# Six buffers for the evictions of one projection unit, and one array for the parked operands of the last units

## The chip, the cores and the metric

The kernel runs on one core of a Trainium2 chip. The metric is the device time of one execution in microseconds; where there are several runs, their median counts. A profile is one execution recorded by the hardware. Its span goes from the first to the last instruction, and the time of the same execution is a little longer.

## What is computed

One inference layer of a streaming encoder, for a prompt of 2048 frames and for 64 frames of a running stream with 4096 past frames. Cut to what matters here:

```python
def layer_inputs(x, norm_g, w_in, b_gate, qn_g, kn_g):
    h = rmsnorm(x, norm_g) @ w_in
    qa, ka, va, za, qb, kb, vb, zb, ga, gb = jnp.split(h, _split_points(), axis=-1)
...
    oa = diff_attn_prompt(qa, ka, va, lam, slopes)
    ob, r_p = retention_prompt(qb, kb, vb, log_g)
    hp = layer_output(hp, oa, ob, za, zb, ga, gb, subln_g[l], lam_init, w_o_diff[l], w_o_ret[l], w_out[l])
```

`h` has 6144 columns. `layer_output` gates the two branches, projects each to 1024 columns, merges them, projects once more and adds `x`.

## The kernel before, in words

**Tiling.** Every matmul operand is split into a high part in the fast format and a low part with the remainder, and each product is made of three matmuls: high by high, high by low, low by high. The prompt is projected in two halves of about 1024 frames. The first half, to about 585 us, uses a Strassen scheme over pairs of blocks. The second half uses, in this order, plain units of 256 columns (`transposed`: weights stationary, frames moving, result with columns on partitions; the first such unit has groups of 256 and 288 frames, the others of 512 and 288), units for k, q and v, and for the last five column groups seven products per group, again after Strassen (`quad`, about 1410 to 1544 us). Attention (`attn_head`: products `s<-K,q`, softmax, `pv<-ath,V`) and the retention steps (`ret_block`: loads `row<-qbT`, `row<-kbT` and `row<-vbN`, then `s<-row`) are interleaved with the second half. After that come the output projections, to the end.

**What sets the order.** The program is written by a planner. Each piece of work is a Python generator that issues instructions and yields the planned time at which it can go on; `loop` takes the ready task with the lowest priority number, and if none is ready it lets the planned TensorE time run forward. The planner adds estimated costs (`P`, `A`, `V`, `G`, `ld`, `st`). TensorE, ACT (ScalarE) and DVE (VectorE) execute in the order in which the planner writes; SP (SyncE, which issues almost all DMAs) and POOL (GpSimd) in the order that the framework makes of it, each a strict queue. Buffers have tags with a fixed number each: `take` waits for the earliest free one, `give` returns it with the time at which it is free. "ev" has three buffers, "tlo" two and "thi" one, all of 128x512.

**What the change touches.** `fin_t` (L1451) evicts a group of a `transposed` unit: it takes a buffer from `q_ev` (L1601), copies the group from its PSUM bank on ACT (`q_copy`, recorded at L1596), returns the bank, stores the buffer to DRAM on SP and returns the buffer when the store should have landed. `mm` has two PSUM banks, so TensorE cannot begin a group before the group two earlier has been copied. The first unit of the second half has eight groups, four of 256 and four of 288 frames; its stores go to `qbT`.

`x_again` (L1480) prepares the operands of the last units while the plain units run. In 20 chunks it forms on POOL the blocks of x (A21, A22, A11, A12 in a "tlo" buffer, called `xa`) and their Strassen sums (S1, S3, S4, S2 in a "thi" buffer, called `xs`), and parks what the seven products need in DRAM: three blocks, three sums, and S2 already split into high and low part. The split goes to a third buffer, an "ev": cast on ACT (L1498), subtraction on DVE (L1503). `x_pass` (L1515) later loads the parked arrays, S2's two parts first, and splits the others itself. `self.parked` becomes 1 when all chunks are parked; from then on `q_ev` may also take "thi" and "tlo".

Of the kernel before, what the change touches and what calls it, by code (L numbers as in the profile page):

```python
# [8 lines left out]
F32 = mybir.dt.float32  # L9
F32R = mybir.dt.float32r  # L10
# [30 lines left out]
SLACK = 400.0  # L41
PACE = 700.0
LATE = 1000.0
# [26 lines left out]


PLAIN = 11
SPREAD = 4000.0
PHASES = [("t2", "S2", "q_p6"), ("b11", "A11", "q_p1"), ("b21", "A12", "q_p2"), ("t1", "S1", "q_p5"),
          ("t3", "S3", "q_p7"), ("t4", "A22", "q_p4"), ("b22", "S4", "q_p3")]
NAMES = ("S1", "S3", "S4", "A22", "A11", "A12")
WIDTH = (256, 288)


# [93 lines left out]
class Hybrid:  # L173
# [123 lines left out]
    def scratch(self):  # L297
        tc = self.tc
        self.qT = [tc.dram_tile([4, 128, TT], F32, name=f"qT{i}") for i in range(2)]
        self.kT = [tc.dram_tile([4, 128, TT], F32, name=f"kT{i}") for i in range(2)]  # L300
        self.vN = [tc.dram_tile([TT, 512], F32, name=f"vN{i}") for i in range(2)]
        self.vsN = tc.dram_tile([NS, 512], F32, name="vsN")
        self.vbN = tc.dram_tile([TT, 512], F32, name="vbN")
        self.qbT = tc.dram_tile([4, 128, TT], F32, name="qbT")
        self.kbT = tc.dram_tile([4, 128, TT], F32, name="kbT")
        self.zaT = tc.dram_tile([4, 128, 8 * GW], F32, name="zaT")
        self.zbT = tc.dram_tile([4, 128, 8 * GW], F32, name="zbT")
        self.gaT = tc.dram_tile([8, 128, 8 * GW], F32, name="gaT")
        self.gbT = tc.dram_tile([8, 128, 8 * GW], F32, name="gbT")
        self.oaT = tc.dram_tile([4, 128, 8 * GW], F32, name="oaT")  # L310
        self.obT = tc.dram_tile([4, 128, 8 * GW], F32, name="obT")
        self.swap = tc.dram_tile([2, 4, 64, 1024], F32, name="swap")
        self.xkeep = tc.dram_tile([128, KC, 128], F32, name="xkeep")
        self.wsum = tc.dram_tile([16, 2, 128, 4, 256], F32, name="wsum")
        self.xd = tc.dram_tile([128, 6, 4, 544], F32, name="xd")
        self.xd2 = tc.dram_tile([128, 2, 4, 544], F32, name="xd2")
        self.mT = tc.dram_tile([8, 2, 128, 8, 128], F32, name="mT")

    def consts(self):
# [1160 lines left out]
    def x_again(self):  # L1480

        nc = self.nc
        yield lambda: "nat1" in self.done
        for g, w in enumerate(WIDTH):
            n = (128, 96)[g]
            for c, a in [(c, a) for c in range(4) for a in range(0, w, n)]:
                yield from self.take("tlo")
                yield from self.take("thi")
                raw, sums = (self.sb(self.ep, [128, 512], tag, name)[:, 0:4 * n].rearrange("p (k t) -> p k t", k=4)
                             for tag, name in (("tlo", "xa"), ("thi", "xs")))  # L1490
                t, t2 = self.x_chunk(g, c, raw, sums, a, n)
                usl = slice(256 * g + a, 256 * g + a + n)
                yield t
                t = self.st(self.xd[:, 3:6, c, usl], raw[:, 1:4], n << 11)
                yield t2
                ev, tag = yield from self.q_ev(2 * n)
                e = ev.bitcast(F32R).rearrange("p (k t) -> p k t", k=2)
                nc.scalar.copy(e[:, 0], sums[:, 3])  # L1498
                t3 = self.A(n, self.pe)
                self.give("tlo", max(t, t2))  # L1500
                t4 = self.st(self.xd[:, 0:3, c, usl], sums[:, 0:3], n << 11)
                yield t3
                nc.vector.tensor_sub(e[:, 1], sums[:, 3], e[:, 0].bitcast(F32))  # L1503
                t = self.V(n + 100, t3)
                self.give("thi", max(t, t4))
                yield t
                self.kept = self.st(self.xd2[:, :, c, usl], e.bitcast(F32), n << 10)
                self.give(tag, self.kept)
                yield self.pe + SPREAD
        self.parked = 1  # L1510

# [3 lines left out]
    def x_pass(self):  # L1515
        self.xslots, self.xfree, self.parked, self.xraw = [], [(1, 0.0)], -1, None
        yield lambda: self.parked == 1 and self.seg1_done is not None
        yield max(self.seg1_done, self.kept)
        for k, (_, name, _) in enumerate(PHASES):
            if k == 0:  # L1520
                for j, x in enumerate(self.x_slot(0)):
                    t = self.ld(x.bitcast(F32), self.xd2[:, j].rearrange("p c t -> p (c t)"), 1114112)
                self.xslots.append((0, t))
                yield lambda: self.xraw is not None
                continue
            t = self.ld(self.xraw, self.xd[:, NAMES.index(name)].rearrange("p c t -> p (c t)"), 1114112)
            s = yield from self.ring(self.xfree)
            yield t
            h, l = self.x_slot(s)
            for c in range(0, 2176, 544):  # L1530
                self.nc.scalar.copy(h[:, c:c + 544], self.xraw[:, c:c + 544])
                t = self.A(544, self.pe)
                yield t
                self.nc.vector.tensor_sub(l[:, c:c + 544], self.xraw[:, c:c + 544], h[:, c:c + 544].bitcast(F32))
                t = self.V(644, t)
            self.xslots.append((s, t))
            yield t
# [61 lines left out]
        return self.A(n, t)  # L1599

    def q_ev(self, n):  # L1601
        tag = yield from self.either(1, "ev", *(("thi", "tlo") if self.parked == 1 else ()))
        return self.sb(self.ep, [128, 512], tag, "ev")[:, :n], tag

    def q_p6(self, q, ps, bank, t, dst, d0, scale, grouped):
# [1601 lines left out]
```

## Time and profile before

| what | value |
|---|---|
| median of 3 runs | 1906.45 us (1902.84 to 1911.58) |
| the profiled execution's own time | 1899.9 us |
| its span | 1897.5 us |
| mean granted TensorE clock | 0.997 |
| busy: TensorE, DVE, ACT, POOL | 1871.9, 1336.5, 973.7, 670.7 us |
| DMA over the span | 340.09 MB, mean 179 GB/s |

Of the profiled execution, 2.4 us lie outside its span. Matmuls overlap: one of 128x288 lasts 0.29 us, but the next starts 0.13 us later. So idle time counts only where TensorE's last matmul has ended. "wh" and "wl" are the high and low part of a weight, "xh" and "xl" of the frames. A number in square brackets in a timeline is the engine's idle time just before the instruction, with what ended it. SPq is SP's queue, and its times are those of issuing a DMA, not of the transfer.

### The profile page before, as it was taken

What the parts mean: (1) busy time and instruction counts of PE and PEld (TensorE: products, weight loads), DVE (VectorE), ACT (ScalarE), POOL (GpSimd) and SP (SyncE); (2) the same over time, 40 slices, a digit from 0 to 9 for tenths busy, and PEclk for the clock granted to TensorE, in tenths of its full rate; (3) what the DMA queues carried; (4) which work ended last, traced back from release to release, by engine and by line L of the source; (5) the groups of instructions that cost most, each with busy time, mean ns of one, the idle gap of its engine ahead of it and who ended that gap; (6) DMA issues with size and microseconds to landing.
All of it is one profiled execution on the core that took longest, in us unless ns stands there. A gap on an engine that the chain in (4) does not pass through costs nothing.

```text
span 1897.5 us, 33103 instructions
## 1 busy us (share of the span) xinstructions
PE 1871.9 (99%) x11090; PEld 1649.4 (87%) x11090; DVE 1336.5 (70%) x3112; ACT 973.7 (51%) x2266; POOL 670.7 (35%) x728
## 2 busy tenths in 40 slices
PE   9999999999998999999999999999999999999999
PEld 7788888888877889888888889899999999999887
DVE  6765757657584777885467677578887969877664
ACT  6434544545434665655455555466666536654221
POOL 2420355554552122121311444431113635522442
PEclk9999999999999999999999999999999999999999
DMA  7664555666757857554622856753534998976542
GB/s 260 209 177 126 162 153 187 179 198 197 249 180 191 233 180 197 158 172 126 189 81 76 224 138 166 177 161 95 136 123 148 279 250 273 274 235 202 177 156 78
DMA packets 402876, 340.09 MB, mean 179 GB/s; under 512 B 85649, under 2 KB 348945, under 8 KB 401682
## 3 DMA queue, kind: packets, MB, share of 16 engines
q1 hardware_dynamic: 402706, 337.98, 60.9%
q8 instruction: 88, 1.44, 0.3%
q14 instruction: 82, 0.67, 0.1%
HBM read 218.27 MB, written 118.75 MB: 178 GB/s over the span
## 4 chain that ended last, share of the span: by engine, by line
PE 88%; DVE 5%; DMA 4%; issue 1%; ACT 1%; SPq 1%; POOL 1%; DVEq 0%; ACTq 0%
PE mm L1138 29%; PE mm L990 8%; PE tp L990 4%; PE at L1996 3%; PE s L1884 2%; PE s L1885 2%; PE s L990 2%; PE mm L1569 2%; PE pv L1976 2%; PE pv L1975 2%; PE pv L1974 2%; PE s L2800 1%; PE s L2799 1%; PE s L2798 1%; SPq L280 1%
## 5 line engine op out<-in xcount | busy, mean ns | idle before, releaser
L749 POOL TENSOR_TENSOR wl<-ws,wh 128x512 fp32r<-128x512 f32 x107 | 149.6, 1409 | 251.8 <-ACT wh L728 243.9
L1138 PE MATMUL mm<-wh,xh 128*128 128x512 f32 x504 | 203.7, 404 | 0.0
L1138 PE MATMUL mm<-wl,xh 128*128 128x512 f32 x504 | 197.9, 393 | 0.8 <-POOL wl L749 0.8
L1138 PE MATMUL mm<-wh,xl 128*128 128x512 f32 x504 | 198.2, 393 | 0.0
L1138 PE MATMUL mm<-xh,wh 128*128 128x288 f32 (+2 forms) x544 | 180.8, 332 | 6.1 <-ACT ev L1596 6.1
L1138 PE MATMUL mm<-xh,wl 128*128 128x288 f32 (+2 forms) x544 | 176.4, 324 | 0.0
L1138 PE MATMUL mm<-xl,wh 128*128 128x288 f32 (+2 forms) x544 | 176.4, 324 | 0.0
L1924 ACT ACTIVATE row<-row,a_mx 128x1024 f32<-128x1024 f32 (+7 forms) x144 | 150.1, 1044 | 9.6 <-DVE a_mx L1903 9.6
L2012 DVE TENSOR_TENSOR atl<-at,ath 128x512 fp32r<-128x512 f32 (+1 forms) x144 | 92.7, 658 | 80.7 <-ACT ath L2010 80.3
L2010 ACT CAST ath<-at 128x512 fp32r<-128x512 f32 (+1 forms) x144 | 79.0, 565 | 106.4 <-PE at L1996 105.1
L857 POOL TENSOR_TENSOR wl<-ws,wh 128x256 fp32r<-128x256 f32 x64 | 55.3, 864 | 197.3 <-ACT wh L848 197.2
L1750 POOL TENSOR_TENSOR r_y<-r_y,r_sq 128x256 f32<-128x256 f32 x32 | 25.9, 808 | 256.9 <-DVE r_sq L1747 159.2
L1893 DVE CUSTOM_DVE_ANT_0 row<-s,dfar 128x512 f32<-128x512 f32 (+2 forms) x149 | 91.3, 629 | 35.5 <-PE s L1885 35.3
L1138 PEld LDWEIGHTS mm<-xh,wh 128*128 128x128 f32 x544 | 103.2, 190 | 13.3 <-ACT ev L1596 6.3
L1138 PEld LDWEIGHTS mm<-wh,xl 128*128 128x128 f32 x504 | 94.6, 188 | 21.7
L1138 PEld LDWEIGHTS mm<-wl,xh 128*128 128x128 f32 x504 | 95.1, 189 | 18.4 <-POOL wl L749 1.1
L1138 PEld LDWEIGHTS mm<-wh,xh 128*128 128x128 f32 x504 | 94.8, 188 | 17.4 <-DVE raw L1309 0.2
L1138 PEld LDWEIGHTS mm<-xl,wh 128*128 128x128 f32 x544 | 103.4, 190 | 6.8
L1138 PEld LDWEIGHTS mm<-xh,wl 128*128 128x128 f32 x544 | 103.2, 190 | 6.8
L1946 DVE SCALAR_TENSOR_TENSOR row<-row,a_w 128x1024 f32<-128x1024 f32 (+5 forms) x88 | 100.6, 1151 | 0.0
L1884 PE MATMUL s<-K,q 128*128 128x512 f32 (+3 forms) x243 | 91.6, 379 | 0.4 <-DVE a_acc L1893 0.4
L728 ACT CAST wh<-ws 128x512 fp32r<-128x512 f32 x111 | 67.0, 619 | 41.6 <-PE mm L1569 8.4
(543 smaller groups left out, 6070.0 us busy)
## 6 DMA issues: line engine op xcount, KB each, us to landing
ws<-in_w_in_dram SPq DMA_DIRECT2D x155, 256.0 KB, 3.5
q<-qT SPq DMA_DIRECT2D x128, 128.0 KB, 3.0
K<-kT SPq DMA_DIRECT2D x48, 256.0 KB, 4.6
V<-vN SPq DMA_DIRECT2D x24, 512.0 KB, 5.3
row<-in_x_prompt_dram SPq DMA_DIRECT2D x16, 512.0 KB, 4.3
wz<-in_w_in_dram SPq DMA_DIRECT2D x32, 256.0 KB, 4.3
row<-in_cache_k_T_dram SPq DMA_DIRECT2D x32, 256.0 KB, 3.1
row<-in_cache_v_diff_dram SPq DMA_DIRECT2D x32, 256.0 KB, 3.6
```

The costliest lines, as they stand in the source:

```text
L728: self.nc.scalar.copy(h, st)
L749: eng.tensor_sub(l, st, h.bitcast(F32))
L857: nc.gpsimd.tensor_sub(l[:, cs], src, h[:, cs].bitcast(F32))
L990: nc.tensor.matmul(ps, w[:, c], xs[x][c], start=bool(tag) and c == 0 and i == 0, stop=c == 3 and i == 2, skip_group_check=True)
L1138: nc.tensor.matmul(ps, p, q, start=c == 0 and i == 0, stop=c == KC - 1 and i == 2)
L1884: nc.tensor.matmul(ps, q1s, kk, start=True, stop=False)
L1893: nc.vector.tensor_tensor_reduce(out=row[:, k0:k0 + n], in0=ps, in1=tab, scale=-SLOPES[h], scalar=3.0e38, op0=ALU.add, op1=ALU.min, accum_ ...
L1924: nc.scalar.activation(u, u, AF.Exp, bias=mx, scale=-1.0, accum_out=lp[:, k:k + 1])
L1946: nc.vector.scalar_tensor_tensor(out=u0, in0=u1, scalar=w[:, 0:1], in1=u0, op0=ALU.mult, op1=ALU.add)
L1996: nc.tensor.transpose(at[:, w:w + 128], src, self.ident)
L2010: nc.scalar.copy(ah[:, :w], at[:, :w])
L2012: nc.vector.tensor_sub(al[:, :w], at[:, :w], ah[:, :w].bitcast(F32))
```

## The change

`q_ev` may take "thi" and "tlo" also while the first transposed unit of the second half is the latest one begun (`self.nplain == 1`), so that unit has six buffers. In `x_again` the "ev" buffer goes: S2's high part is cast over A21, which nothing needs after the sums, its low part replaces S2 in place, and each of the two buffers is stored whole, in one DMA. The parked arrays become one of eight, with new names in order. The pause between two chunks is 6000 ns in the planner's time, not 4000, and buffers come back 1000 ns later in its reckoning (`LATE`).

```diff
-SPREAD = 4000.0
+SPREAD = 6000.0
...
-NAMES = ("S1", "S3", "S4", "A22", "A11", "A12")
+NAMES = ("S2h", "A22", "A11", "A12", "S1", "S3", "S4", "S2l")
...
-        self.xd = tc.dram_tile([128, 6, 4, 544], F32, name="xd")
-        self.xd2 = tc.dram_tile([128, 2, 4, 544], F32, name="xd2")
+        self.xd = tc.dram_tile([128, 8, 4, 544], F32, name="xd")
...
                 t, t2 = self.x_chunk(g, c, raw, sums, a, n)
                 usl = slice(256 * g + a, 256 * g + a + n)
+                yield t2 + SLACK
+                hi = raw[:, 0].bitcast(F32R)
+                nc.scalar.copy(hi, sums[:, 3])
+                t = self.A(n, t2)
                 yield t
-                t = self.st(self.xd[:, 3:6, c, usl], raw[:, 1:4], n << 11)
-                yield t2
-                ev, tag = yield from self.q_ev(2 * n)
-                e = ev.bitcast(F32R).rearrange("p (k t) -> p k t", k=2)
-                nc.scalar.copy(e[:, 0], sums[:, 3])
-                t3 = self.A(n, self.pe)
-                self.give("tlo", max(t, t2))
-                t4 = self.st(self.xd[:, 0:3, c, usl], sums[:, 0:3], n << 11)
-                yield t3
-                nc.vector.tensor_sub(e[:, 1], sums[:, 3], e[:, 0].bitcast(F32))
-                t = self.V(n + 100, t3)
-                self.give("thi", max(t, t4))
-                yield t
-                self.kept = self.st(self.xd2[:, :, c, usl], e.bitcast(F32), n << 10)
-                self.give(tag, self.kept)
+                nc.vector.tensor_sub(sums[:, 3].bitcast(F32R), sums[:, 3], hi.bitcast(F32))
+                t2 = self.V(n + 100, t)
+                for k, x, tag, t in ((0, raw, "tlo", t), (4, sums, "thi", t2)):
+                    if t > self.pe:
+                        yield t
+                    self.kept = self.st(self.xd[:, k:k + 4, c, usl], x, n << 11) + LATE
+                    self.give(tag, self.kept)
                 yield self.pe + SPREAD
...
-        tag = yield from self.either(1, "ev", *(("thi", "tlo") if self.parked == 1 else ()))
+        tag = yield from self.either(1, "ev", *(("thi", "tlo") if self.parked == 1 or self.nplain == 1 else ()))
```

Since buffers come free at other planned times, the planner writes another order from the first unit on. TensorE's order is the same until about the middle of its matmuls and differs in 83 places after that, until the last units are done; SP's differs from the first unit on. Three places matter for the prediction. In the rows, a number behind a name tells apart buffers or loads with one name, and "x2" means twice in a row.

The first place is ACT's queue in the first unit: its second to fifth copy, with the semaphores that each waits for (PE is TensorE, DMAHW a DMA). Before:

```order
L1596 COPY ev_6239<-mm_6171 128x256 [waits DMAHW5_49,DMAHW2_49,PE_49]
L1596 COPY ev_6267<-mm_6230 128x256 [waits DMAHW3_49,PE_49,Activation_49]
L1596 COPY ev_6301<-mm_6269 128x256 [waits DMAHW2_49,PE_49,Activation_49]
L1596 COPY ev_6329<-mm_6303 128x288 [waits DMAHW7_49,PE_49,Activation_49]
L1924 ACTIVATE row_6182,a_lp_6359<-row_6182,a_acc_6349 128x128 [waits DVE_49]
```

Now:

```order
L1591 COPY ev_6229<-mm_6170 128x256 [waits PE_49]
L1591 COPY ev_6266<-mm_6231 128x256 [waits DMAHW4_49,DMAHW0_49,PE_49]
L1591 COPY ev_6300<-mm_6268 128x256 [waits DMAHW5_49,DMAHW2_49,PE_49]
L1591 COPY ev_6328<-mm_6302 128x288 [waits DMAHW3_49,PE_49]
L1919 ACTIVATE row_6182,a_lp_6358<-row_6182,a_acc_6348 128x128 [waits DVE_49]
```

Before, the fourth copy (`ev_6301`) takes the buffer of the second (`ev_6239`) and waits for that one's store. Now it takes a buffer of the first half, whose store to `gbT` stands ahead of all loads of the first head; the first, second and sixth copy take "thi" and "tlo" buffers.

The second place is SP's queue in the same unit, from the store of the third copy on. `K` and `q` are loads for the first head, `q_6382` (now `q_6381`) the third set. Before:

```order
L285 DMA qbT_65<-ev_6267 128x256
L285 DMA gbT_70<-ev_6127 128x2x256
L285 DMA qbT_65<-ev_6301 128x256
L280 DMA K_6528<-kT0_59 64x1024
L285 DMA qbT_65<-ev_6329 128x32
L285 DMA qbT_65<-ev_6329 128x256
L280 DMA q_6382<-qT0_57 64x2x256 x2
L280 DMA q_6382<-qT1_58 64x2x256 x2
```

Now:

```order
L285 DMA qbT_65<-ev_6266 128x256
L285 DMA gbT_70<-ev_6126 128x2x256
L285 DMA qbT_65<-ev_6300 128x256
L285 DMA qbT_65<-ev_6328 128x32
L285 DMA qbT_65<-ev_6328 128x256
L280 DMA q_6381<-qT0_57 64x2x256 x2
L280 DMA q_6381<-qT1_58 64x2x256 x2
```

The stores of the fifth copy and the third set of q moved ahead of a K load; the rows ahead of these are the same.

The third place is in the attention stage, where before, at about 1220 us, ACT waits for an "ev" buffer. ACT's queue there before (`ath` is the high part of the attention weights, which `pv` needs; the CAST `ev<-xs` is a parked chunk's):

```order
L1498 CAST ev_13861<-xs_13779 128x96
L1924 ACTIVATE row_6182,a_lp_13849<-row_6182,a_mx_13798 128x1024
L1596 COPY ev_13876<-mm_13826 128x512
L1596 COPY ev_13914<-mm_13879 128x288
L2010 CAST ath_13957<-at_13952 128x512
L2010 CAST ath_13966<-at_13961 128x512
```

And now, at the same groups of that unit:

```order
L1591 COPY ev_13785<-mm_13749 128x288
L2005 CAST ath_13808<-at_13803 128x512
L2005 CAST ath_13827<-at_13822 128x512
L2005 CAST ath_13863<-at_13858 128x512
L1494 CAST xa_13812<-xs_13813 128x96
L2005 CAST ath_13879<-at_13874 128x512
```

The chunk's cast no longer takes an "ev". SP's queue at this place, before and now (`row<-qbT`, `row<-kbT` and `row<-vbN` are the loads of a retention step):

```order
L285 DMA zbT_68<-ev_13824 128x4x8
L285 DMA zbT_68<-ev_13824 128x256
L285 DMA xd_76<-xs_13779 128x3x96
L280 DMA row_6182<-qbT_65 128x4x128
L280 DMA row_6182<-kbT_66 128x4x128
L280 DMA row_6182<-vbN_64 128x512
```
```order
L285 DMA xd_76<-xa_13664 128x4x96
L285 DMA xd_76<-xs_13665 128x4x96
L285 DMA zbT_68<-ev_13745 128x2x256
L280 DMA row_6182<-qbT_65 128x4x128
L280 DMA row_6182<-kbT_66 128x4x128
L280 DMA row_6182<-vbN_64 128x512
```

The store for which `ev_13914` waited (`ev_13824`) stood just ahead of these loads; now the evictions there wait for stores that are written out further ahead of these loads. Where the whole program is written out, the first matmul that reads these loads (`s<-row`) comes 20 matmuls behind them before; now none stands between.

More of the change, by code (lines that the diff above doesn't have):

```diff
@@ L1521, in x_pass @@
                 for j, x in enumerate(self.x_slot(0)):
-                    t = self.ld(x.bitcast(F32), self.xd2[:, j].rearrange("p c t -> p (c t)"), 1114112)
+                    t = self.ld(x.bitcast(F32), self.xd[:, 7 * j].rearrange("p c t -> p (c t)"), 1114112)
                 self.xslots.append((0, t))
```

## The prediction

> **What bounds the kernel now.** I read four views, in this order: the page's first lines, TensorE's waits, the timelines of the engines at each wait, and the granted clock by stretches.
>
> ```profile
> span 1897.5 us, 33103 instructions
> PE 1871.9 (99%) x11090; PEld 1649.4 (87%) x11090; DVE 1336.5 (70%) x3112; ACT 973.7 (51%) x2266; POOL 670.7 (35%) x728
> ```
>
> TensorE is busy for 1871.9 of 1897.5 us, and both programs give it the same number of matmuls. So the change can pay only through the 25.6 us in which TensorE stands idle and through stretches in which its clock is halved. Next, who made TensorE wait (line, releaser: total us, times, longest):
>
> ```profile
> PE mm L1138 <- ACT ev L1596: 6.1, 1, 6.1
> PE s L2341 <- DMA row<-kbT: 2.9, 1, 2.9
> PE at L1569 <- DVE ev L1589: 2.4, 2, 1.4
> PE pv L1974 <- ACT ath L2010: 1.9, 1, 1.9
> ```
>
> The first row is the second half's first transposed unit. The ACT timeline says what its eviction waited for:
>
> ```profile
> 594.48 0.37 ACT L1596 COPY ev<-mm 128x256 f32<-128x256 f32 x1 [0.62 <-ACT ev L1596]
> 606.15 0.37 ACT L1596 COPY ev<-mm 128x256 f32<-128x256 f32 x1 [11.30 <-DMA qbT<-ev]
> ```
>
> The fourth copy found no free "ev" buffer until a store of an earlier one had landed. SP's timeline shows why that store was late:
>
> ```profile
> 595.25 2.56 SPq L280 DMA_DIRECT2D q<-qT  x4
> 597.91 0.54 SPq L280 DMA_DIRECT2D ws<-in_w_in_dram  x1
> 598.49 3.31 SPq L280 DMA_DIRECT2D q<-qT  x4
> 601.90 0.54 SPq L285 DMA_DIRECT2D qbT<-ev  x1
> ...
> 604.88 2.98 SPq L285 DMA_DIRECT2D qbT<-ev  x1
> 607.97 0.36 SPq L285 DMA_DIRECT2D gbT<-ev  x1
> 608.44 0.44 SPq L285 DMA_DIRECT2D qbT<-ev  x1
> 608.92 0.47 SPq L280 DMA_DIRECT2D K<-kT  x1
> 612.33 0.81 SPq L285 DMA_DIRECT2D qbT<-ev  x2
> 613.24 2.54 SPq L280 DMA_DIRECT2D q<-qT  x4
> ```
>
> The copy was made by 593.9, but its store is issued at 601.90, behind the loads of K and q for the first head. On TensorE, and in the chain (start, us, what):
>
> ```profile
> 600.17 0.29 PE L1138 MATMUL mm<-xh,wl 128*128 128x288 f32 x1
> 606.58 0.61 PE L1138 MATMUL mm<-xh,wh 128*128 128x288 f32 x1 [6.11 <-ACT ev L1596]
> ...
> 618.15 0.39 PE L1885 MATMUL tp<-K,q 128*128 128x256 f32 x1 [0.43 <-DMA q<-qT]
> ```
> ```profile
> 601.90 4.15 DMA qbT<-ev
> 615.17 2.93 DMA q<-qT
> ...
> 1099.95 4.88 DMA row<-kbT
> ```
>
> The wait costs more than 6.11 us. In these stretches (us, busy time and instructions of PE, PEld, DVE, ACT, POOL, then clock, DMA share, GB/s) the clock column falls to 0.50 behind it:
>
> ```profile
> 600.40:605.60 5.20, 0.07 (x1) 0.00 (x0) 0.00 (x0) 0.00 (x0) 0.00 (x0) 1.00 1.12 256
> 605.60:612.40 6.80, 5.82 (x25) 5.83 (x26) 1.03 (x6) 0.87 (x3) 0.00 (x0) 0.50 1.15 346
> ...
> 1219.80:1223.40 3.60, 1.49 (x11) 1.05 (x10) 1.45 (x3) 1.38 (x3) 1.71 (x5) 1.00 0.95 259
> 1223.40:1226.80 3.40, 3.40 (x19) 3.40 (x18) 1.68 (x8) 0.55 (x2) 2.41 (x5) 0.50 1.12 301
> ...
> 1101.90:1105.00 3.10, 0.23 (x2) 0.06 (x1) 2.85 (x6) 0.00 (x0) 1.63 (x1) 1.00 0.87 244
> ```
>
> From 606.58 to 612.40 TensorE works at half speed, 5.8 us for 2.9 us of work. The first wait thus costs 6.1 + 2.9 = 9.0 us.
>
> **Term A, the first unit.** With six buffers the fourth copy takes a buffer whose last store left before the loads, so the matmuls go on at 600.3. What is late next are the q loads. TensorE's work from 606.58 to 617.7 (618.15 less the 0.43 us wait) is 11.1 us, 8.2 us at full clock, which would bring it to the matmul of 618.15 at 608.5. On the way it needs the second set of four q loads, issued by 601.80; the store issued behind them landed at 601.90 + 4.15 = 606.05, so they cost up to 2.5 us; I take 2 and arrive at 610.5. There it needs the third set. Before, that set was issued at 613.24, because SP waited until 612.33 for the fifth copy. In the new order it stands in front of the K load, behind two stores whose copies are done by then. SP is still at the store of 604.88 until 607.86, which the change does not move: then 0.95 us for the next two stores, 0.81 for the two after them, and 2.54 for the four loads, the last of them issued at about 611.6. With the 2.93 us of the chain it lands at 614.6; with DMA at a share of 1.15 I take 615.0. So TensorE gets past this point 3.1 us earlier instead of 9.0, after a new wait of about 4.5 us. The clock was halved behind the waits of 6.11 and of 1.89 us, for 6.8 and 3.4 us, so I count half clock again, some 4 us of it, a loss of 2. A = 1.1 us; ends: a loss of 0.5 if the loads land at 615.8 and the clock stays down for 6.8 us (2.9), and the whole 9.0 if the loads aren't late.
>
> **Term B, ev buffers in the attention stage.** ACT's queue, TensorE and SP at the fourth wait of the list:
>
> ```profile
> 1221.03 0.40 ACT L1596 COPY ev<-mm 128x288 f32<-128x288 f32 x1 [8.72 <-DMA zbT<-ev]
> ...
> 1221.97 0.39 PE L1974 MATMUL pv<-ath,V 128*128 128x256 f32 x1 [1.89 <-ACT ath L2010]
> ...
> 1228.19 0.55 PE L2346 MATMUL at<-ident,row 128*128 128x128 f32 x3 [0.67 <-DVE atl L2012]
> ...
> 1219.67 0.56 SPq L280 DMA_DIRECT2D row<-kbT  x1
> ```
>
> An eviction waits 8.72 us for an "ev" buffer, and the two casts of "ath" that TensorE needs stand behind it in ACT's queue. One of the three buffers was held by parked high and low parts. In the new order parked chunks take no "ev" buffer, and no eviction there follows the store that it needs so closely. That removes 1.89 + 0.67 and half of the 3.4 us at clock 0.50, together 4.3 us. But the new order has at this place a retention step whose three row loads are written out directly ahead of its first matmul, with no matmul between (before: 20). SP issues them ahead of time only as far as it has got ahead. Such a load took 4.88 us, so TensorE waits between 0 and 4.88, and at the upper end with half clock behind it. The nearest row is the same kind of wait, 2.87 us at 1104.97, behind which the clock stayed at 1.00 (stretch 1105.00 to 1108.50 below). I take 2.9: B = 1.4; ends -2.3 (4.3 - 4.88 - 1.7) and 4.3.
>
> ```profile
> 1104.97 1.13 PE L2341 MATMUL s<-row 128*128 128x128 f32 x8 [2.87 <-DMA row<-kbT]
> 1105.00:1108.50 3.50, 3.50 (x30) 3.50 (x31) 0.02 (x1) 0.48 (x1) 1.42 (x2) 1.00 0.76 246
> ```
>
> **Term C, the retention step at 1104.97.** Its kbT load was written out 38 matmuls ahead; in the new order the loads of the step that takes this place stand 71 matmuls or more ahead. At 0.12 us and more per matmul that is over 4 us more cover, so the 2.87 us go. Against it stands a later step with only 18 matmuls behind its qbT load, for which I deduct 0.9 (bounds 0 and 2.9, this same row). C = 2.0; ends 0 and 2.9.
>
> **What costs nothing.** The parked chunks keep their cast and their subtraction (20 of each, 276 and 268 ns), and three stores become two:
>
> ```profile
> L1498 ACT CAST ev<-xs x20: 254/276/313, 1050.2 to 1284.9; 128x96 fp32r<-128x96 f32 x12, 128x128 fp32r<-128x128 f32 x8
> L1503 DVE TENSOR_TENSOR ev<-xs,ev x20: 250/268/1196, 1050.5 to 1286.6; 128x96 fp32r<-128x96 f32 x12, 128x128 fp32r<-128x128 f32 x8
> L285 SPq DMA_DIRECT2D xd<-xa x20: 359/374/853, 940.5 to 1255.2; - x20
> L285 SPq DMA_DIRECT2D xd<-xs x20: 359/369/440, 944.9 to 1276.8; - x20
> L285 SPq DMA_DIRECT2D xd<-ev x20: 525/556/629, 1053.9 to 1286.9; - x20
> L280 SPq DMA_DIRECT2D xl<-xd x1: 346/346/346, 1375.9 to 1375.9; - x1
> ```
>
> SP saves between 0.19 us (1.30 less two of 0.556) and 0.56 us (less two of 0.37) per chunk, 4 to 11 us over 350 us; SP runs beside TensorE and gains only lead. The wider spacing, 2 us more by the planner in each of 20 chunks, can move the last store from 1286.9 to about 1327. The reload starts at 1375.9, so 49 us of cover are left; if a later end used them up, the wait would fall on the first of the last four units' matmuls. Until parking ends, evictions have three buffers, but no longer share them. The waits of 2.4 us for DVE in the last units of this half I leave as they are: 0, ends -2.4 and 2.4.
>
> **Sum.** 1.1 + 1.4 + 2.0 = 4.5 us. The profiled execution took 1899.9 us (span 1897.5): 1895.4 after. It lies 6.5 us under the median of the three runs, 1906.45, so in the terms of the median I forecast **1902.0 us**.
>
> **Rivals.**
> - All three waits go and nothing follows: 9.0 + 4.3 + 2.9 = 16.2 us, 1883.7 in this execution, 1890.3 as a median. For it: buffers are what the first and fourth wait lacked. Against it: DMA shares of 1.12 and 1.15 around the first one; the loads cannot come much sooner. Chance 0.20.
> - Slower: at the retention step of term B SP is not ahead at all. TensorE waits 4.88 us and loses 2.9 at half clock, as behind the first wait: 7.8 against 4.3 removed. With A and C at nothing that is 3.5 us more, 1903.4, as a median 1910. It decides as soon as the load is issued less than 0.6 us (4.88 - 4.3) ahead of its matmul. For it: at 1219.67 SP was in step with TensorE, not ahead. Against it: the stores in front of those loads no longer wait for a parked low part. Chance 0.14.
> - The extra buffers are not free in time, and the fourth copy waits as before: 1899.9, as a median 1906.5. Against it: in the new order the copies that use them show no wait for a DMA. Chance 0.06.
> - The clock stays up behind the new wait, so that A is 3.1: the sum is 6.5 us, 1893.4, as a median 1900.0. For it: behind 1101.90 to 1105.00, with 0.23 us busy of 3.10, it stayed at 1.00. Against it: at 1223.40 it fell with 1.49 us of 3.60 busy. Chance 0.12.
>
> [...]
>
> **Numbers.** The forecast's chance is 0.48. A difference of 0.5% (9.5 us) is about what a measurement of this kernel can tell from no change. The first rival alone passes it on the fast side, 0.20, with 0.03 from the forecast's tail: faster 0.23. The slower rival reaches 3.5 us by itself and passes 0.5% only together with a new wait in the last units: 0.07. Within: 0.70. The range goes from the first rival, 1890, to the slower one with 2 us of the spread of single runs, 1912.
>
> **What would show it.** A right: no wait at the sixth group of matmuls of the first unit, a wait of 3 to 5 us for "q<-qT" near 610 to 615, and clock 0.50 behind it; wrong if TensorE passes that load without a wait. B right: no "ath" wait behind an eviction, and a wait of 1 to 4 us for "row<-kbT" near 1220. C right: no wait for rows near 1100. Wrong as a whole if new waits, in the last units above all, add up to more than 9 us.

## The result and the profile after

The changed kernel takes 1898.81 us (median of 10 executions, 1897.45 to 1902.98) against 1903.9 us of the kernel before (10 executions): ratio 0.9973, 95% interval 0.996 to 0.9985. That is 5.1 us less; the interval goes from 2.9 to 7.6. In a later comparison the ratio was 0.996 (0.9947 to 0.9973). One execution of the kernel before (6561.56 us) and one of b_only (4763.15 us), more than twice as long as any other, are left out below.

The two profiled executions differ by much less: 1899.9 us before, 1898.9 after. The page's first lines of the changed kernel:

```profile
span 1897.1 us, 33035 instructions
PE 1872.0 (99%) x11090; PEld 1648.1 (87%) x11090; DVE 1332.9 (70%) x3111; ACT 972.9 (51%) x2266; POOL 673.1 (35%) x729
```

TensorE's idle time went from 25.6 to 25.1 us, but it is made up of other waits (line, what ended the wait: total us, times, longest):

```profile
PE tp L1879 <- DMA q<-qT: 3.8, 1, 3.8
PE mm L1564 <- DVE ev L1584: 2.9, 4, 1.2
PE mm L1564 <- DVE u L1584: 1.6, 2, 1.0
PE s L2336 <- DMA row<-kbT: 1.6, 1, 1.6
...
PE s L2336 <- DMA row<-qbT: 1.2, 1, 1.2
...
PE s L1564 <- DVE ev L1584: 1.0, 1, 1.0
```

The wait of 6.1 us for ACT's eviction, the 2.9 us for rows near 1102 and the 1.9 us for "ath" are gone. New are 3.8 us for the third q set, 1.6 and 1.2 us for rows, and 5.5 us for VectorE in the last units of the second half (L1564; before 3.0: 2.4 + 0.6).

**The first unit.** ACT's fourth and fifth copies are now released by TensorE, no longer by a store:

```profile
598.55 0.37 ACT L1591 COPY ev<-mm 128x256 f32<-128x256 f32 x1 [2.51 <-PE mm L1137]
601.74 0.40 ACT L1591 COPY ev<-mm 128x288 f32<-128x288 f32 x1 [2.82 <-PE mm L1137]
```

SP's queue there; the store of 2.94 us and the loads behind it stand in the forecast's order, 1 to 2 us later:

```profile
604.70 1.00 SPq L280 DMA_DIRECT2D V<-vN  x2
605.89 2.94 SPq L285 DMA_DIRECT2D qbT<-ev  x1
...
611.20 2.53 SPq L280 DMA_DIRECT2D q<-qT  x4
```

TensorE stands still in front of the third set, and behind it the clock is at half for one stretch of 3.4 us. The stretches here are cut at the clock's two changes, 617.05 and 620.47, and ahead of them at the same length (us; busy time of PE, PEld, DVE, ACT, POOL; clock, DMA share, GB/s):

```profile
606.82:610.23 3.41, 3.27 (x21) 3.12 (x22) 2.75 (x13) 1.45 (x4) 0.00 (x0) 1.00 1.13 339
610.23:613.64 3.41, 1.62 (x13) 1.38 (x11) 0.88 (x6) 1.68 (x6) 0.00 (x0) 1.00 1.15 333
613.64:617.05 3.41, 0.93 (x5) 0.79 (x6) 0.18 (x1) 0.00 (x0) 0.00 (x0) 1.00 0.90 233
617.05:620.47 3.42, 3.42 (x16) 3.42 (x15) 2.52 (x12) 0.54 (x2) 0.00 (x0) 0.50 0.80 180
```

**The attention stage.** At the place of the "ath" wait TensorE now waits for the rows of a retention step, and 36 us later for those of the step with the short lead:

```profile
1215.24 1.02 PE L2336 MATMUL s<-row 128*128 128x128 f32 x7 [1.56 <-DMA row<-kbT]
...
1251.16 1.02 PE L2336 MATMUL s<-row 128*128 128x128 f32 x7 [1.25 <-DMA row<-qbT]
```

The clock stays at 1.00 behind both (from 620.47 to 1897.05). It does not in every execution: in a second profile of the changed kernel (after_again) the first of these waits is 2.19 us, and half clock follows.

```profile
1213.10:1216.50 3.40, 1.21 (x11) 1.00 (x10) 0.84 (x3) 1.25 (x3) 3.32 (x8) 1.00 0.78 195
1216.50:1219.90 3.40, 3.40 (x18) 3.40 (x18) 0.20 (x1) 0.07 (x1) 2.29 (x8) 0.50 0.62 166
```

**The last units.** The same 100 us, before and after:

```profile
1430.00:1530.00 100.00, 97.01 (x769) 95.71 (x768) 82.77 (x130) 60.18 (x118) 55.18 (x38) 1.00 0.79 232
```
```profile
1430.00:1530.00 100.00, 94.32 (x737) 91.78 (x737) 75.74 (x125) 56.61 (x108) 50.15 (x36) 1.00 0.73 215
```

TensorE is idle for 3.0 us of them before and for 5.7 after.

### The profile page after: what moved, and what is told of

Read it like the earlier page. It is cut to its first block, busy times and chain, and to the rows that moved or that the text cites. A ratio compares the mean times of both kernels' runs of the same rounds, so it can differ in the third digit from the quotient of the medians.

```text
span 1897.1 us, 33035 instructions
## 1 busy us (share of the span) xinstructions
PE 1872.0 (99%) x11090; PEld 1648.1 (87%) x11090; DVE 1332.9 (70%) x3111; ACT 972.9 (51%) x2266; POOL 673.1 (35%) x729
## 4 chain that ended last, share of the span: by engine, by line
PE 89%; DVE 4%; DMA 4%; SPq 1%; ACT 1%; issue 1%; POOL 0%; DVEq 0%; POOLq 0%; ACTq 0%
PE mm L1137 29%; PE mm L989 8%; PE tp L989 4%; PE at L1991 3%; PE s L1880 2%; PE s L1879 2%; PE s L989 2%; PE mm L1564 2%; PE pv L1971 2%; PE pv L1970 2%; PE pv L1969 2%; DMA q<-qT 1%; PE s L2793 1%; PE s L2795 1%; PE s L2794 1%; PE pv L2257 1%
## 5 line engine op out<-in xcount | busy, mean ns | idle before, releaser
L1879 PE MATMUL s<-K,q 128*128 128x512 f32 (+3 forms) x243 | 91.8, 379 | 0.6 <-DMA q<-qT 0.4
L1880 PE MATMUL s<-K,q 128*128 128x512 f32 (+3 forms) x243 | 88.3, 365 | 0.9 <-DMA q<-qT 0.9
```

What stands on the lines that cost most here:

```text
L1879: nc.tensor.matmul(ps, q1s, kk, start=True, stop=False)
L1880: nc.tensor.matmul(ps, q2s, kk, start=False, stop=True)
```

## The experiments

"Lost" below is (1 - mean granted clock) x span, averaged over the executions: at most so much time went to half clock. Ratios are to the kernel before, run on the same chip at the same time; a to c mark the three groups of runs. A ratio need not equal the ratio of two medians: for b_only it gives 4.0 us less than before, the medians 5.5. So a difference of 1 or 2 us between two rows says little.

| kernel | ratio (95%) | mean clock | lost, us |
|---|---|---|---|
| before (a, b, c) | 1 | 0.9956, 0.9952, 0.9951 | 8.3, 9.1, 9.3 |
| a_only (a) | 0.9996 (0.9985 to 1.0006) | 0.9959 | 7.8 |
| b_only (a) | 0.9979 (0.997 to 0.9988) | 0.9979 | 4.0 |
| before_s6000 (a) | 0.9978 (0.9969 to 0.9986) | 0.9975 | 4.8 |
| after_s4000 (a) | 0.9956 (0.9943 to 0.9969) | 0.9978 | 4.1 |
| fill_q (b) | 0.9955 (0.9942 to 0.9968) | 0.9993 | 1.3 |
| v_later (b) | 0.9992 (0.9984 to 1.0001) | 0.9960 | 7.6 |
| wo_pool (b) | 0.9986 (0.9976 to 0.9997) | 0.9963 | 7.0 |
| after_again (c) | 0.996 (0.9947 to 0.9973) | 0.9983 | 3.2 |
| p_only (c) | 0.9955 (0.9943 to 0.9968) | 0.9972 | 5.4 |
| fill_s4000 (c) | 0.9967 (0.9955 to 0.9979) | 0.9982 | 3.4 |
| wo_dve (c) | 0.9974 (0.9965 to 0.9982) | 0.9976 | 4.7 |

### Taking the change apart

**a_only**, the six buffers alone, on the kernel before:

```diff
-        tag = yield from self.either(1, "ev", *(("thi", "tlo") if self.parked == 1 else ()))
+        tag = yield from self.either(1, "ev", *(("thi", "tlo") if self.parked == 1 or self.nplain == 1 else ()))
```

> The kernel before with the six buffers in the first unit alone; the parked operand as before, so TensorE's, VectorE's and GpSimd's orders are those of before. Theory (the parts are separate, and each is worth what the two profiles show at its place): no wait for the eviction at the sixth group of matmuls, a wait of 3 to 4.5 us for the third q set near 611 to 615 with half clock behind it, about 1.4 us gained by the retention of the unit's end, and the waits of 2.9 us (row loads near 1102) and 1.9 us (ath near 1220) still there: about 1.4 us less than before, ratio 0.999. Rival (the first wait costs more in most executions than in the profiled one, with more stretches at half clock behind it): this edit alone carries most of the 5 us that the medians differ by, ratio 0.9975 or lower.

Measured: 0.8 us less, not to be told from none. The wait for the eviction is gone and one of 4.9 us for the third q set stands in its place (3 to 4.5 were expected), with 6.8 us at half clock behind it. The same profile shows what half clock does in an execution of the old order: a wait of 2.2 us for rows near 1102, which in the first profile left the clock alone, pulls it down here.

```profile
609.70:613.10 3.40, 0.47 (x4) 0.23 (x2) 0.00 (x0) 0.52 (x2) 0.00 (x0) 1.00 0.96 294
613.10:616.50 3.40, 1.34 (x4) 1.10 (x5) 0.19 (x1) 0.00 (x0) 0.00 (x0) 0.50 0.72 198
616.50:619.90 3.40, 3.40 (x16) 3.40 (x15) 2.59 (x12) 0.40 (x1) 0.00 (x0) 0.50 0.73 163
...
1101.20:1104.60 3.40, 1.18 (x8) 0.75 (x7) 3.37 (x7) 0.45 (x1) 1.27 (x1) 1.00 1.01 283
1104.60:1108.00 3.40, 3.40 (x18) 3.40 (x17) 0.00 (x0) 0.00 (x0) 1.95 (x3) 0.50 0.78 257
```

The theory holds for the place, and its gain of 1.4 us lies within the interval; the rival (this edit carries the medians) falls.

**b_only**, the rest of the change, without the six buffers:

```diff
-        tag = yield from self.either(1, "ev", *(("thi", "tlo") if self.parked == 1 or self.nplain == 1 else ()))
+        tag = yield from self.either(1, "ev", *(("thi", "tlo") if self.parked == 1 else ()))
```

> The changed kernel without the six buffers in the first unit; TensorE's, VectorE's and GpSimd's orders are those of the changed kernel. Theory (separate parts): the wait of about 6 us for the eviction near 600 is back, with 3.4 to 7 us at half clock behind it; in the attention stage, 1060 to 1360 us, it gains 4 to 5 us as the changed kernel did, and gives 3 to 4 us back in the last units (waits for VectorE between 1430 and 1530); in all 0.5 to 1.5 us less than before, ratio 0.9995. Rival (the attention stage carries the gain in the medians): ratio 0.9975. Rival 2 (order luck: the losses in the last units are jitter of one execution and not of this order): the VectorE waits between 1430 and 1530 sum to under 4 us, as before, not 6 to 7.

Measured: 4.0 us less than before. The first wait is back with 5.9 us. The profiled execution, 1902.58 us, is one of the two longest of eleven; over all of them the ratio is 0.9979, the first rival's number. Less time at half clock, 4.0 us instead of 8.3, makes up most of it; where in the program that was, one profile can't tell. The VectorE waits of the last units come back as in the changed kernel (6.1 us by the list of waits), so they belong to this order; rival 2 falls.

**before_s6000**, the spacing alone:

```diff
-SPREAD = 4000.0
+SPREAD = 6000.0
```

> The kernel before with the wider spacing alone, 6000. Theory: the first unit as before (wait of 6 us and half clock), the attention stage in a new order; the ev buffers stay shared with parked parts, so an ath wait behind a blocked eviction can still occur; waits in the attention stage between 3 and 8 us in all, the time within 3 us of before, ratio 0.9985 to 1.0015. Rival (the wider spacing, and not the buffers, is what ends the ath and row waits): the attention stage gains 4 us or more, ratio 0.998 or lower.

Measured: 4.2 us less. The rival's number is met, and so is what it says of the waits: with the old buffers and nothing but the wider spacing the "ath" wait does not appear, and of the row waits 0.8 us is left, while the waits for VectorE in the last units grow to 5.2 and 1.8 us:

```profile
PE mm L1138 <- ACT ev L1596: 5.9, 1, 5.9
PE s L1569 <- DVE ev L1589: 5.2, 3, 2.6
PE mm L1569 <- DVE u L1589: 1.8, 2, 1.3
...
PE s L2341 <- DMA row<-kbT: 0.8, 1, 0.8
```

**after_s4000**, the changed kernel with SPREAD back at 4000, and **p_only**, the same without the six buffers (the line of b_only): of the change only the parked operand's new places are left in it.

> The changed kernel with the old spacing of the parked chunks, 4000 in place of 6000: another order from the attention stage on, the first unit as in the changed kernel. Theory: the spacing by itself saves nothing; what the attention stage and the last units cost goes by how far ahead row loads and evictions happen to be written: the first unit as changed (a q wait of 3 to 4.5 us), no eviction wait for a parked buffer in front of ath, other waits of 2 to 6 us in all between 1090 and 1300; within 3 us of the changed kernel, ratio to before 0.996 to 0.999. Rival (chunks spaced too tightly hold thi and tlo and block evictions): an ev or ath wait of 2 us or more in the attention stage comes back, ratio 0.9985 to 1.0005.

> The parked operand's new places alone: the old spacing of 4000, three buffers in the first unit. Theory (the three edits are not additive: the new places and the wider spacing each end the same waits in the attention stage, the six buffers give 0.7 to 1.1 us): ratio to before 0.9955 to 0.997, that is 6 to 9 us less than before, and no wait of over 1 us between 1060 and 1360. Rival (0.9956 with the six buffers was luck of the first unit): ratio 0.998.

Measured: 8.4 us and 8.6 us less than before. No wait over 0.2 us is left between 1060 and 1360 in either profile, also without the wider spacing, so both rivals fall. The theory of p_only holds. That of after_s4000 was too careful: it expected 2 to 6 us of such waits and a ratio of 0.996 or more. So the edits do not add: the new places alone are worth 8.6 us (group c), the spacing alone 4.2 us (a), both together 4.0 us (a, b_only). In group a the wider spacing, added to the new places, seems to cost 3 us or so: b_only stands 4.4 us over after_s4000 (3.5 by the medians), of which the six buffers may explain 1. In group c the changed kernel and p_only cannot be told apart, so no version is shown to beat the changed kernel.

### The new wait in the first unit

**v_later**: the first head's V loads are written out behind the third q set.

```diff
             self.heads.append(hd)
+            yield lambda: self.nq > 2
...
         self.qs.append((q, t))
+        self.nq += 1
```

> The changed kernel with the first head's two V loads written out behind the third q set instead of ahead of it. Theory (the third q set comes late because SP is throttled and the DMA engines are full of K and V in front of it): SP issues the set 2 to 4 us earlier, the wait of 3.8 us for it falls to 0 to 2 us, and the clock stays up; 2 to 4 us less than the changed kernel, ratio to before 0.995 to 0.9965; V is needed only some 10 us later. Rival (the set is bound to its buffer, which the first set leaves only when its last matmul is done, or to transfers other than V): it lands at the same time, 615 us, and the wait stays at 3.5 us or more.

SP now issues the set at 607.02 instead of 611.20, and the three stores in front of it take 1.60 us together, where one alone took 2.94:

```profile
605.00 1.60 SPq L285 DMA_DIRECT2D qbT<-ev  x3
607.02 2.54 SPq L280 DMA_DIRECT2D q<-qT  x4
609.61 1.22 SPq L280 DMA_DIRECT2D V<-vN  x2
```

The wait of 3.8 us shrinks to 0.7, and the clock stays up there (1.00 from 609.7 to 616.5). From the 2601st matmul, near 563 us, to the last of the first transposed unit, the 2918th, TensorE takes 54.6 us here; with the six buffers and V ahead it takes 59.4 to 60.5 in six profiles (59.4 in both of the changed kernel), with the old buffers 60.5 to 62.5 in five. So the theory of the wait is shown. The forecast of the total fails: ratio 0.9992. The planner writes another order from there on, with other waits, and half clock takes 7.6 us on average:

```profile
PE s L2338 <- DMA row<-qbT: 3.3, 1, 3.3
PE s L2671 <- DVE ga L2684: 2.8, 1, 2.8
PE tp L1719 <- DVE r_hi L1711: 2.7, 1, 2.7
PE s L2338 <- issue: 1.7, 1, 1.7
```

**fill_q**: matmuls on data that is there fill the wait; the order is otherwise kept.

```diff
+                if (h, p, b, c, ci) == (0, 2, 0, 0, 0):
+                    for _ in range(30):
+                        nc.tensor.matmul(ps, kk[:, 0:128], kk, start=True, stop=True)
```

> The changed kernel with 30 matmuls of 128x256 on data that is there already (about 0.12 us each, 3.6 us in all) in front of the matmul that waits for the third q set; the output is unchanged, since the real matmul overwrites them. Theory (the clock falls because TensorE had nothing to do in that wait): TensorE stays busy over the 3.8 us, no stretch at half clock between 612 and 630, mean granted clock up by 0.001 to 0.002, the end of the first unit 1.7 to 3.4 us earlier than in the changed kernel; ratio to before 0.995 to 0.9965. Rival (the halving follows something else, such as the burst of transfers): the stretch at half clock stays where it was, the time is that of the changed kernel, ratio 0.9973, or later if the filling outlasts the wait.

```profile
610.70:614.90 4.20, 4.14 (x35) 3.93 (x33) 0.00 (x0) 0.60 (x2) 0.00 (x0) 1.00 0.92 276
614.90:618.30 3.40, 2.36 (x16) 2.22 (x17) 1.54 (x9) 0.24 (x1) 0.00 (x0) 1.00 0.84 222
1212.20:1215.60 3.40, 1.41 (x13) 1.17 (x11) 0.69 (x1) 0.44 (x1) 2.20 (x7) 1.00 1.02 275
1215.60:1219.10 3.50, 2.62 (x13) 2.65 (x13) 0.99 (x2) 1.25 (x3) 2.33 (x5) 0.51 0.49 127
```

The clock stays at 1.00 through both stretches, although the DMA engines are still busy for 0.92 and 0.84 of them. In the changed kernel it also stayed up in the stretch with a share of 1.13, where TensorE was busy (606.82), and fell behind one with 0.90, where it was not (613.64). So in these stretches half clock went with idle TensorE, not with the share of the transfers. Mean clock 0.9993, the highest of all kernels. The stretch from the 2601st matmul to the unit's last takes 58.5 us, 0.8 less than in the changed kernel's two profiles, with the filling; 1.7 to 3.4 were expected. The ratio of 0.9955 is where the theory put it, but its interval overlaps both of the changed kernel's. In the profiled execution, the longest of its six (1901.51 us), the time gained came back as a longer wait for rows at 1213 (2.9 us instead of 1.6), with the clock at half behind it.

**fill_s4000**: the same fill in after_s4000.

> The changed kernel with the old spacing of 4000 and the 30 filling matmuls in front of the matmul that waits for the third q set. Theory (idle TensorE costs a second time through the clock, and the two gains add): mean clock 0.999 or more, 2 to 3 us less at half clock than with the spacing alone, ratio to before 0.993 to 0.995. Rival (what the fill saves is given back at a later wait for a load that then has not landed, as in the changed kernel with the fill, where the wait for rows near 1213 grew from 1.6 to 2.9 us): ratio 0.995 to 0.9965.

Measured: 0.9967, the rival's case. The clock is no better than with the spacing alone (3.4 us lost against 4.1), and in its profile the last units and the first output matmuls are slower: one wait there for VectorE ("ga") is 3.9 us long, 3.1 us in after_s4000 and p_only. That this alone takes back what the first unit gains is not shown.

### The last units

**wo_pool** and **wo_dve**: the low parts of w_o, one in three of them on GpSimd in the changed kernel, go all to GpSimd, or all to VectorE:

```diff
-                self.spawn(self.split_fin("oz", h[:, :, sl], l[:, :, sl], s, t, (kp + q) % 3 == 0, slot, q), 2)
+                self.spawn(self.split_fin("oz", h[:, :, sl], l[:, :, sl], s, t, True, slot, q), 2)
```

(False in the second.)

> The changed kernel with the low parts of w_o in the last units all on GpSimd instead of one in three. Theory (in the last units VectorE sets the pace: evictions that TensorE waits for stand behind low parts of 0.7 to 1.8 us): the waits for VectorE between 1430 and 1530 fall from about 6.7 us to under 4, 2 to 4 us less than the changed kernel, ratio to before 0.995 to 0.9965. Rival (the evictions there wait for stores of ev buffers or for other low parts, of xl): the waits stay at 5 us or more, the time within 1 us of the changed kernel.

> The changed kernel with the low parts of w_o in the last units all on VectorE (before one in three on GpSimd). Theory (VectorE's subtractions there take 0.7 us beside an idle GpSimd and up to 1.8 us beside a busy one, so that work on GpSimd costs VectorE as much as its own): the subtractions of xl and w_o average nearer to 0.9 us than 1.1, the waits for VectorE between 1430 and 1530 fall from 6.7 to under 5 us, ratio 0.5 to 2 per mille under that of the changed kernel on this chip. Rival (six more subtractions on VectorE are simply six more ahead of the evictions): the waits stay or grow, ratio the same or higher.

What an eviction stands behind there, in the changed kernel's VectorE queue:

```profile
1500.45 1.10 DVE L2626 TENSOR_TENSOR ogl<-on,ogh 128x528 fp32r<-128x528 f32 x1
1501.47 1.82 DVE L1529 TENSOR_TENSOR xl<-xraw,xh 128x544 fp32r<-128x544 f32 x1
...
1507.21 1.77 DVE L2477 TENSOR_TENSOR w_o_retl<-wst,w_o_reth 128x512 fp32r<-128x512 f32 x1
1508.90 0.41 DVE L1584 TENSOR_TENSOR ev<-mm,u 128x256 f32<-128x256 f32 x1
```

The low parts of xl, from 1430 to 1530, in wo_pool and in wo_dve (1103 ns in the changed kernel):

```profile
L1529 DVE TENSOR_TENSOR xl<-xraw,xh 128x544 fp32r<-128x544 f32 x20 | 23.1, 1156 | 0.5 <-ACT xh L1526 0.5
```
```profile
L1529 DVE TENSOR_TENSOR xl<-xraw,xh 128x544 fp32r<-128x544 f32 x20 | 19.7, 987 | 1.0 <-ACT xh L1526 1.0
```

With less on GpSimd VectorE's subtractions of xl get shorter, with more on it longer, so that part of the theory holds. The waits hardly answer, and both forecasts of them fail: 5.5 us for VectorE in the changed kernel, 4.6 in wo_pool with a new one of 1.9 us behind it ("ga", L2669), 5.3 in wo_dve. Neither ratio is better than the changed kernel's two. That VectorE's load sets the pace here is not shown; which of its instructions would have to move stays open.

### More executions of both kernels

**before_again** and **after_again** are the two kernels unchanged.

> The kernel before, for one more profile. Theory (most executions of it spend more time at half clock than the profiled one did: mean clock 0.9956 over 28 runs, 8.3 us lost, against 0.9981 and 3.6 us for the changed kernel): two to three stretches of 3.4 us at half clock besides the one behind the first wait, behind the waits near 1102, 1220 or 1507; time 1901 to 1907. Rival (the profiled execution was typical and the spread comes from elsewhere): half clock behind the first and the fourth wait alone, 10.2 us in all, and a time above 1902 that the waits explain.

> The changed kernel once more, on the same chip as the next three, as their common measure. Ratio to before 0.996 to 0.9985 as measured first; mean granted clock 0.998 against 0.995 to 0.996 of before, so that the time lost at half clock is 3 to 4 us less than before and the remaining time within 1 us of it. Rival (the clock differed by the chip and not by the order): the clock is that of before on this chip, and the ratio nearer to 1.

before_again took 1901.72 us. Half clock behind the first wait (6.8 us, and 3.4 us more behind two waits for q of about 1 us each at 616 to 618) and behind the "ath" wait near 1221; near 1102 and 1507 the clock stayed up this time. So the theory holds in the amount, two stretches besides the first, and only in part in the places: which waits pull the clock down changes from one execution to the next.

```profile
1101.40:1104.90 3.50, 2.28 (x13) 1.65 (x12) 3.50 (x10) 1.32 (x3) 0.00 (x0) 1.00 0.82 222
1104.90:1108.30 3.40, 2.42 (x20) 2.44 (x21) 1.47 (x5) 0.00 (x0) 1.29 (x1) 1.00 0.81 241
...
1220.90:1224.30 3.40, 0.83 (x5) 0.53 (x5) 0.98 (x2) 1.38 (x3) 1.30 (x4) 1.00 0.97 269
1224.30:1227.70 3.40, 3.40 (x18) 3.40 (x18) 2.16 (x9) 0.27 (x1) 2.82 (x6) 0.50 1.08 304
```

after_again, on the same chip as 16 executions of before: means 1898.2 against 1905.6 us, 7.4 us apart, of which up to 9.3 - 3.2 = 6.1 us is half clock. That is more than the 3 to 4 us of its theory, and 1.3 us are left where it allowed 1; in kind it holds. The rival falls, since both ran on one chip. (For the first ten executions the clock of the kernel before is not recorded, so the split is made here.)

## Why the prediction came out as it did

The forecast, 1902.0 us in a range of 1890 to 1912, lies 3.2 us over the measured median; the change it spoke of, 4.5 us less, stands against 5.1. The sum was closer than its parts, and that is partly luck: D below cost time that the sum did not have, and less half clock, which it had only in part, gave about as much back. The 9.5 us that it took for the least difference to be told was too careful: the interval of 0.996 to 0.9985 leaves out 1.

- **A, the first unit: right.** Forecast a new wait of about 4.5 us for the third q set, half clock behind it, 1.1 us gained. The profile shows 3.79 us and one stretch at half clock (1.7 us lost instead of 2). Over all six profiles with the six buffers the wait is 3.5 to 4.9 us long, and in four of them two windows of this unit run at half clock, 6.8 us. Over the stretch named at v_later the five profiles with the old buffers average 61.2 us and the six with the new ones 60.1: 1.1 us less. The executions can't confirm an amount so small: the 0.8 us of a_only are not told from none, the intervals of the changed kernel and b_only overlap, and p_only, without the six buffers, is no slower than the changed kernel.
- **B, the "ath" wait: the place right, the cause not settled.** The wait for the eviction is gone, and a wait for rows stands at the retention step without lead: 1.56 us instead of 2.9, clock up. In after_again it is 2.19 us with half clock behind it, so the price that the forecast took, 2.9 us, was near the mark there. But before_s6000 loses the "ath" wait too, with parked parts still in "ev" buffers. So a shared buffer can make the wait, and another order alone, as that of before_s6000, can move it away.
- **C, rows near 1102: right.** None there; the step with 18 matmuls of lead costs 1.25 us (0.9 was deducted; in after_again it is 0.89, in b_only, with the same order, 2.0 us with half clock behind it).
- **D, the last units: wrong.** "The waits of 2.4 us for DVE in the last units of this half I leave as they are: 0, ends -2.4 and 2.4." TensorE's idle time from 1430 to 1530 grew by 2.7 us, more than the end of 2.4. It did not grow by chance of one execution: from 1430 to 1575 TensorE is idle for 3.0 to 3.6 us in the three profiles of the old order (before, before_again, a_only) and for 4.4 to 9.0 us in the eleven of new orders, with the wider spacing and without it. So what was gained in the attention stage was in part given back here. From the 5500th matmul to the 9100th, where B, C and D lie, the first pair of profiles gains 1.4 us, where B and C were to give 3.4.
- **The step from one execution to the median: wrong.** The forecast took the 6.5 us between the profiled execution and the median as fixed. 2.6 of them came from a median of only three runs: with ten it is 1903.9 instead of 1906.45, and that alone is most of the 3.2 us by which the forecast was too high. Of the rest, much is half clock. The profiled execution of before was a lucky one: its stretches at half clock come to 6.0 us lost, where 28 others average 1904.5 us and 8.3 lost, so that 2.3 of the 4.6 us between them are half clock. For the changed kernel the profiled execution lies at its median (1898.9 and 1898.81), although with 1.7 us lost against 3.6 on average it was lucky too; so the clock does not explain the whole offset. Behind the waits near 1102, 1220 and 1507 the clock fell in some of the profiled executions: to 0.50 for 3.4 us each behind the first and the third in a_only, and behind the second in before and before_again; in before it stayed at 1.00 behind the first and the third. The change takes the first of these away and puts another in the place of the second. Term C was counted at full clock because that one execution showed it so.
- **The wider spacing was put at nothing.** It is not: alone it is worth 4.2 us. The three buffers are still shared in that kernel, so the likely way is the other order; that is argued, not tried apart.

In the pair of profiles D and two things that the forecast did not have ate the gain: 0.8 us of a wait for VectorE at 280 us, ahead of the change, and 1.0 us in the output stage (below). So the profiled execution came out 3.5 us over its forecast (1895.4), and the median 3.2 us under: errors of opposite sign, in D and these two things and in the offset.

Of the rivals, neither the full gain nor the buffers that are not free in time occurred; "the clock stays up" falls (617.05 to 620.47 at 0.50). The slower one does not occur: SP was late for its rows by 1.56 us, not by 4.88.

## What to carry to other kernels

In this kernel a wait had two prices, its length and the clock behind it, and both changed from one execution of a kernel to the next: the wait for rows near 1215 took 1.56 us with the clock at 1.00 behind it (after), and 2.19 us with 3.4 us at 0.50 behind it (after_again). So take the mean clock of many executions of the kernel before you explain a difference of a few us, and don't carry the gap between one profiled execution and the median over to another kernel. Where a planner orders the work, an edit's direct effect (4.8 us in v_later) can be smaller than what the new order does elsewhere; try the edit's parts and a neutral shift of the order, as the spacing here, before you credit its mechanism. When a stage is sped up, look at who sets the pace of the next one.

## What the runs showed of the hardware

**The clock behind TensorE's waits.** In the profiles of the two kernels, without the first and the last 10 us of the program, the clock is at 0.50 from 605.59 to 612.41 and from 1223.40 to 1226.81 (before), and from 617.05 to 620.47 (after). These are 6.827, 3.413 and 3.413 us, and the 610.986 us between the first two are 179 times 3.413. I cut both profiles on from these changes at 3.413 us. The ten stretches at full clock in which TensorE was least busy, and the clock in the next stretch:

| profile, start of the stretch | busy share of TensorE | clock behind it |
|---|---|---|
| before, 602.17 | 0.00 | 0.50 |
| after, 613.64 | 0.27 | 0.50 |
| before, 1219.99 | 0.38 | 0.50 |
| before, 1100.52 | 0.46 | 1.00 |
| after, 610.23 | 0.48 | 1.00 |
| before, 598.76 | 0.50 | 1.00 |
| before, 1506.71 | 0.55 | 1.00 |
| after, 1507.93 | 0.57 | 1.00 |
| before, 1510.12 | 0.58 | 1.00 |
| after, 1248.52 | 0.63 | 1.00 |

In other profiles the clock was at about 0.50 behind 1.18 and 1.17 us busy of 3.40 (a_only, from 1101.20 and 1507.40), 1.21 of 3.40 (after_again, 1213.10), 0.83 of 3.40 (before_again, 1220.90) and 1.41 of 3.40 (fill_q, 1212.20). Of the four stretches at half clock in before and after, one was busy for 0.71 of its time, and another at half came behind it (before, 605.59); the three that were busy throughout had full clock behind them. At 0.50, 3.413 us hold 1.7 us of work less than at 1.00. The table is no rule: by the count over all 14 profiles, 4 of 36 stretches at full clock that were busy for 0.46 to 0.64 had half clock behind them too, and what set them apart I can't say.

**VectorE beside GpSimd.** Low parts of xl (both inputs in SBUF) took 0.71 us on average where GpSimd did nothing meanwhile (10 in the changed kernel) and 1.83 us where it was busy all the while (2; in the kernel before 1.4 us, 7, of which two took 0.71 us all the same), while evictions with one input from TensorE's banks took 0.43 us in both cases in the changed kernel.

**A slower output stage.** From matmul 9100 to matmul 10750 the same matmuls take 240.17 us before, in a_only and in after_s4000, but 241.17 in the changed kernel, 241.18 in after_again and b_only: about 0.6 ns on each, without a wait. In these six profiles it goes with the order, not with the execution; the cause was not tried and stays open.
